# A decoder block in split fp32: left sides of the first products and value weights moved, output projection in order, three gate and up products begun ahead

## The chip, the core and the metric

The kernel runs on one core of one Trainium2 chip. The core has five engines with an instruction queue each: TensorE (PE, matrix products), VectorE (DVE), ScalarE (ACT), GpSimd (POOL) and SyncE (SP), which here issues nearly all DMAs. Each engine takes its instructions strictly in the order in which they were issued; semaphores make it wait for the others. The metric is the device time of one execution in microseconds (us), lower is better.

## What is computed

One layer of a decoder block on 1024 tokens of width 1024, all in float32:

```
h = rmsnorm(x, norm_mix)
qa, ka, va, qb, fb, ib, gb, gate_a, gate_b = split(h @ w_in)
ya = dilated_attention(qa, ka, va)              # 8 heads of 64, three windows
yb = hgrn2(qb, fb, ib, gb, lb, hg_norm)         # 4 heads, chunks of 64
x = x + (sigmoid(gate_a) * (ya @ w_a_up) + sigmoid(gate_b) * (yb @ w_b_up)) @ w_out
g, u = split(rmsnorm(x, norm_ffn) @ w_gu)       # 2 x 2816 wide
x = x + (silu(g) * u) @ w_down
x = x + (p @ w_pe) * sigmoid(rmsnorm(x, norm_ple) @ w_pg)
out = rmsnorm(x, norm_final)
```

## The kernel before

**Numbers.** Every float32 operand of a matrix product is split into a high and a low part (a cast to fp32r, and the difference). A product of two such operands is three matmuls: hi with hi, hi with lo, lo with hi. A split of a weight or an activation is a cast on ACT (or on POOL for `wr`, in `weight`) and a subtraction on DVE.

**Units.** Most projections (10 units) and gate and up (22 units) use Strassen's scheme in Winograd's form, in `winograd`. A unit covers two blocks of weights; it has seven products, always in the order 1, 5, 7, 2, 3, 4, 6, each of 12 matmuls with 512 columns (four blocks of the contraction, three matmuls for each). The generator `lefts` loads a unit's two weights (`w0`, `w1`, on SP), builds the sums s1 to s4 and splits the seven left sides into `q` (cast L299, difference L300); a pool of five buffers lets it run that far ahead. The right sides are made once, from the activations, and are used by all units: `right_b11` (product 1), `right_t1` (5), `right_t3` (7), `right_b21` (2), `right_b22` (3), `right_t4` (4), `right_t2` (6). Each of them ends in `block`: a cast on ACT (L235) and a difference on DVE (L236). T3 needs a difference on POOL (L249), T2 another (L261), T1 and T4 one on DVE (L245, L262). In PSUM a unit's products share banks: product 2 is added to the bank of product 1, after ACT has copied product 1 to `m` (L333), and DVE reads a bank for the sums `v` and `u` (L335, L337) before the next use of it.

**The program in time.** (1) The start, up to 56 us: the activation x arrives in eight tiles `xr`, is scaled by the norm's gains and split (`xh`, `xl`), and its squares are summed in `sqs`; meanwhile five tiles of gates are computed directly (`start`). The norm's factor is `rstd_rep`: an fp32 matmul of `ones` with the sums into a bank (`ms`, L209), two reads of this bank by ACT (L210, L211; the first needs its table of functions), three steps on DVE. (2) The ten projection units, 56 to 264 us; their right sides are made by `start_rights`, which first scales `xr` in place (L376). (3) Attention, from 264 us: queries and keys come back from DRAM (`qr`, `kl`) and are split (`q`, `kh`, `kl`); the value product is `v_gemm` (L484 to L486), with weights `wr` split to `wh` and `wl`; scores are `sp` (L525, L526), their row maxima come from DVE (L538), the exponential from ACT (L542). A `Filler` puts steps of gate products between the scores. (4) The recurrence, the merge. (5) The output projection, to 875 us: for each of eight blocks d it computes x1, writes it, scales it to `xg`, and makes the right sides of gate and up as they become possible. (6) Gate and up, 22 units of some 19 us. Beside them SP, DVE and `down_sums` prepare left sides of the down projection (`ls`, stored to `s_dram`). (7) The down projection, (8) the last stage.

**What sets the order.** Code is written stage by stage, and a scheduler of the tile framework merges it to one order for each engine; `tc.issue_after(i)` holds what is recorded inside it behind the instruction i. Memory is given by numbered slots: `ring([41])` is a buffer in slot 41, and a new tile in it waits until the readers of the old one are done.

## Time and profile before

| | |
|---|---|
| median of three runs | 1650.5 us (1648.26 to 1650.99) |
| the profiled execution, its own time | 1653.13 us |
| its span, first to last instruction | 1651.3 us |
| busy: PE, DVE, ACT, POOL | 97%, 68%, 39%, 29% |
| mean granted clock of PE | 0.987 of full |
| read from and written to HBM | 164.16 and 62.39 MB |

The span is that of one profiled execution; all times inside it count from its start. A busy share is a mean over all stages: what a change in one stage is worth is read from that stage. A waiting PE is seen by the idle time ahead of one of its instructions, with the instruction of another engine that released it. The granted clock is the share of the full 2.4 GHz that PE was given in a stretch; its two levels are 1.0 and 0.5 (1.2 GHz).

### The profile page before, as it was taken

What the parts mean: (1) busy time and instruction counts of PE and PEld (TensorE: products, weight loads), DVE (VectorE), ACT (ScalarE), POOL (GpSimd) and SP (SyncE); (2) the same over time, 40 slices, a digit from 0 to 9 for tenths busy, and PEclk for the clock granted to TensorE, in tenths of its full rate; (3) what the DMA queues carried; (4) which work ended last, traced back from release to release, by engine and by line L of the source; (5) the groups of instructions that cost most, each with busy time, mean ns of one, the idle gap of its engine ahead of it and who ended that gap; (6) DMA issues with size and microseconds to landing.
All of it is one profiled execution on the core that took longest, in us unless ns stands there. A gap on an engine that the chain in (4) does not pass through costs nothing.

```text
span 1651.3 us, 21727 instructions
## 1 busy us (share of the span) xinstructions
PE 1599.5 (97%) x7968; PEld 1334.9 (81%) x7968; DVE 1119.2 (68%) x1725; ACT 651.9 (39%) x1130; POOL 475.7 (29%) x357
## 2 busy tenths in 40 slices
PE   8899998999999999999998999999999999999996
PEld 7687776898897888888786878888888788878886
DVE  8855655568665567774648786667777757789536
ACT  6422333357653011532336333333333454454433
POOL 2555662223322111015353222223333201002214
PEclk9999998999999999999999999999999999999998
DMA  5233344223224232543434773224444677765102
GB/s 199 77 103 113 128 147 140 80 87 81 65 71 156 91 108 98 177 145 118 134 127 144 269 260 130 90 101 142 153 160 159 214 262 249 237 200 159 43 1 102
DMA packets 93419, 227.97 MB, mean 138 GB/s; under 512 B 10368, under 2 KB 19840, under 8 KB 93312
## 3 DMA queue, kind: packets, MB, share of 16 engines
q1 hardware_dynamic: 93168, 226.57, 41.3%
q8 instruction: 62, 1.02, 0.3%
q14 instruction: 45, 0.37, 0.1%
q10 hardware_dynamic: 144, 0.02, 0.0%
HBM read 164.16 MB, written 62.39 MB: 137 GB/s over the span
## 4 chain that ended last, share of the span: by engine, by line
PE 47%; DVE 6%; DMA 5%; issue 2%; POOL 1%; ACT 1%; SPq 0%; DVEq 0%; POOLq 0%
PE u L275 7%; PE u L276 7%; PE u L277 7%; PE mm L192 5%; PE mm L194 5%; PE mm L193 5%; PE dnb L275 2%; PE dnb L277 2%; PE dnb L276 2%; DVE B L236 1%; DMA s_dram<-ls 1%; PE g L666 1%; DMA ls<-w_dn 1%; DMA w<-s_dram 1%; DMA w<-w_dn 1%
## 5 line engine op out<-in xcount | busy, mean ns | idle before, releaser
L275 PE MATMUL u<-B,q 128*128 128x512 f32 x776 | 303.9, 394 | 8.3 <-ACT m L333 5.1
L276 PE MATMUL u<-B,q 128*128 128x512 f32 x776 | 304.3, 392 | 3.9 <-DVE B L236 3.9
L277 PE MATMUL u<-B,q 128*128 128x512 f32 x776 | 303.6, 391 | 2.9 <-DVE q L300 2.9
L275 PEld LDWEIGHTS u<-B,q 128*128 128x128 f32 x776 | 146.8, 189 | 44.1 <-ACT m L333 9.5
L276 PEld LDWEIGHTS u<-B,q 128*128 128x128 f32 x776 | 146.6, 189 | 35.3 <-DVE B L236 5.4
L277 PEld LDWEIGHTS u<-B,q 128*128 128x128 f32 x776 | 146.7, 189 | 34.1 <-DVE q L300 3.3
L192 PE MATMUL mm<-xh,wh 128*128 128x512 f32 (+1 forms) x352 | 138.6, 394 | 0.0
L299 ACT CAST q<-s 128x512 fp32r<-128x512 f32 x128 | 79.4, 622 | 148.9 <-PE u L277 132.9
L300 DVE TENSOR_TENSOR q<-s,q 128x512 fp32r<-128x512 f32 x128 | 107.3, 841 | 40.9 <-ACT q L299 40.1
L194 PE MATMUL mm<-xh,wl 128*128 128x512 f32 (+1 forms) x352 | 132.3, 376 | 0.1
L193 PE MATMUL mm<-xl,wh 128*128 128x512 f32 (+1 forms) x352 | 131.8, 374 | 0.0
L171 POOL TENSOR_SCALAR wh<-wr 128x1024 fp32r<-128x1024 f32 (+1 forms) x55 | 59.9, 1091 | 247.6 <-PE mm L193 104.7
L300 DVE TENSOR_TENSOR q<-w,q 128x512 fp32r<-128x512 f32 x96 | 91.9, 958 | 51.1 <-ACT q L299 51.0
L192 PE MATMUL mm<-h,wh 128*128 128x512 f32 (+1 forms) x296 | 114.7, 387 | 1.2 <-POOL wh L171 1.1
L193 PE MATMUL mm<-l,wh 128*128 128x512 f32 (+1 forms) x296 | 114.4, 386 | 0.9 <-DVE l L910 0.9
L194 PE MATMUL mm<-h,wl 128*128 128x512 f32 (+1 forms) x296 | 113.7, 385 | 0.0
L299 ACT CAST q<-w 128x512 fp32r<-128x512 f32 x96 | 59.7, 622 | 122.0 <-PE u L277 69.7
L544 POOL TENSOR_SCALAR p<-p,rd 128x128 f32<-128x128 f32 (+3 forms) x64 | 53.3, 835 | 143.3 <-DVE rd L543 123.8
L1103 POOL TENSOR_TENSOR us<-v 128x512 f32<-128x512 f32 x22 | 38.4, 1746 | 171.6 <-DVE v L337 158.7
L194 PEld LDWEIGHTS mm<-xh,wl 128*128 128x128 f32 x352 | 66.8, 190 | 12.0 <-DVE wl L172 0.5
L484 PE MATMUL mm<-wh,xh 128*128 128x256 f32 x256 | 76.4, 300 | 0.0
L294 POOL TENSOR_TENSOR s<-s,w 128x512 f32<-128x512 f32 x32 | 45.1, 1410 | 107.4 <-DVE s L292 88.2
(305 smaller groups left out, 3791.5 us busy)
## 6 DMA issues: line engine op xcount, KB each, us to landing
w<-w_gu SPq DMA_DIRECT2D x44, 512.0 KB, 3.9
t_dram<-t SPq DMA_DIRECT2D x44, 256.0 KB, 2.3
w<-w_in SPq DMA_DIRECT2D x20, 512.0 KB, 3.8
w<-w_dn SPq DMA_DIRECT2D x40, 256.0 KB, 3.3
st<-t_dram SPq DMA_DIRECT2D x20, 512.0 KB, 4.5
ls<-w_dn SPq DMA_DIRECT2D x32, 256.0 KB, 4.1
wr<-w_in SPq DMA_DIRECT2D x13, 512.0 KB, 3.7
sg_dram<-gt SPq DMA_DIRECT2D x24, 256.0 KB, 2.0
```

The lines of the kernel that those rows point to most:

```text
L171: pool.tensor_scalar(hi, raw, 1.0, 0.0, ALU.mult, ALU.add)
L192: pe.matmul(dst, hi[:, k, :], xh[:, c0 : c0 + n], start=first and k == ks[0], stop=False)
L193: pe.matmul(dst, hi[:, k, :], xl[:, c0 : c0 + n], start=False, stop=False)
L194: pe.matmul(dst, lo[:, k, :], xh[:, c0 : c0 + n], start=False, stop=last and k == ks[-1])
L275: pe.matmul(dst, q[:, 0, k], bh, start=first and not more and k == 0, stop=False, skip_group_check=more)
L276: pe.matmul(dst, q[:, 0, k], bl, start=False, stop=False, skip_group_check=more)
L277: pe.matmul(dst, q[:, 1, k], bh, start=False, stop=end, skip_group_check=more)
L294: pool.tensor_sub(s2, s1, a11)
L299: act.copy(q[:, 0], left[m])
L300: dve.tensor_sub(q[:, 1], left[m], f32(q)[:, 0])
L484: pe.matmul(b, xh[:, ts_], hi[:, k % 4, :], start=(k == 0), stop=False)
L544: pool.tensor_scalar(pr[:, :n], pr[:, :n], rd, 0.0, ALU.mult, ALU.add)
```

## The change

Five things are changed; all matmuls of products are the same.

1. At the start ACT scales all eight `xr` in a row, and the right sides of product 5 and of product 7 are made behind them, with POOL's differences for T2 directly between and behind those for T3. The norm's `rstd_rep` is recorded after these, behind `right_read` and `right_made`.
2. The first value weights `w_v0` are loaded and split during the last projection unit, in slots 41 to 44. The first pair of score rows is held behind the last matmul of the first value product (`values_made`).
3. The output projection takes its blocks d in the order 0 to 7 rather than 0, 4, 1, 5, 2, 6, 3, 7. For d under 4 the right sides of products 1 and 5 are made, for the others that of 7 and T2's difference, and the squares follow behind POOL's last instruction.
4. Gate and up's left sides are pinned ahead of the right sides of products 2, 3, 4 and 6 (`ffn_lead`), with product 1's left side of the second unit taken third (`early`). Products 1 and 5 of the first unit and product 1 of the second are issued before product 7.
5. The norm's two sums for gate and up go to a bank of their own tag, `b1`.

```diff
@@ -276,16 +276,29 @@
...
             pe.matmul(dst, q[:, 1, k], bh, start=False, stop=end, skip_group_check=more)
-    def winograd(units, qr, sr, after=(), eng=pool):
+    def winograd(units, qr, sr, after=(), eng=pool, early=False):
         def lefts():
-            for src0, src1, n in units:
-                w0, w1 = RAW.next([P, 2 * n, P], F32, "w0"), RAW.next([P, 2 * n, P], F32, "w1")
-                nc.sync.dma_start(w0, src0)
-                nc.sync.dma_start(w1, src1)
+            def load(src, n, name):
+                w = RAW.next([P, 2 * n, P], F32, name)
+                nc.sync.dma_start(w, src)
+                return w
+            def split_left(x, n):
+                q = qr.next([P, 2, n, P], F32R, "q")
+                act.copy(q[:, 0], x)
+                dve.tensor_sub(q[:, 1], x, f32(q)[:, 0])
+                return q
+            second = None
+            for i, (src0, src1, n) in enumerate(units):
+                w0 = second if early and i == 1 else load(src0, n, "w0")
+                w1 = load(src1, n, "w1")
                 a11, a12, a21, a22 = w0[:, :n], w0[:, n:], w1[:, :n], w1[:, n:]
@@ -294,11 +307,11 @@
...
                 left = {1: a11, 2: a12, 3: s4, 4: a22, 5: s1, 6: s2, 7: s3}
-                for m in ORDER:
-                    q = qr.next([P, 2, n, P], F32R, "q")
-                    act.copy(q[:, 0], left[m])
-                    dve.tensor_sub(q[:, 1], left[m], f32(q)[:, 0])
-                    yield q
+                for m in ORDER[1:] if early and i == 1 else ORDER:
+                    yield split_left(left[m], n)
+                    if early and i == 0 and m == ORDER[1]:
+                        second = load(units[1][0], n, "w0")
+                        yield split_left(second[:, :n], n)
         left_gen, ahead, unit_gen = chain(lefts(), after), [], iter(enumerate(units))
@@ -360,7 +373,7 @@
...
     for _ in range(WARM):
-        pe.matmul(warm[:, :P], ones, ones, start=True, stop=True)
+        warm_up = pe.matmul(warm[:, :P], ones, ones, start=True, stop=True)
     w_start = [weight_parts(a["w_in"][20 + t], [P, KD, P]) for t in range(NTOGETHER)]
@@ -372,9 +385,10 @@
     def start_rights(j, i):
-        for k in {5: (i,), 7: (i + 4,)}.get(j, ()):
-            act.activation(xr8[k], xr8[k], AF.Identity, scale=vec[:, V_MIX + k : V_MIX + k + 1])
-        right[j][i] = RIGHT[j](xr8, i, 4, ring([TB[j][i]]))
+        t2 = (xr8[i + 4][:, c1],) if j in (4, 6) else ()
+        right[j][i] = RIGHT[j](xr8, i, 4, ring([TB[j][i]]), *t2)
+    pe_engine, pool_engine = warm_up.ins.engine, nc.gpsimd.engine
     def latest(engine):
@@ -416,19 +430,31 @@
...
             dve.tensor_copy(lmask, lm)
-    rs = ring([46]).next([P, S], F32, "rs")
-    t1, t2 = TMP.next([P, S], F32, "t"), TMP.next([P, S], F32, "t")
-    for c in range(2):
-        cs = slice(c * 512, c * 512 + 512)
-        scale_read, _ = rstd_rep(rs[:, cs], sqs[:, cs], MS.next([P, 512], F32, "ms"), 1.0 / D, t1[:, cs], t2[:, cs])
     with tc.issue_after(last_sum.ins):
...
     with tc.issue_after(last_split), tc.issue_after(last_square.ins):
+        for k in range(KD):
+            act.activation(xr8[k], xr8[k], AF.Identity, scale=vec[:, V_MIX + k : V_MIX + k + 1])
+        scaled = latest(act_engine)
+    with tc.issue_after(scaled):
+        for j in (5, 7):
+            for i in range(4):
+                start_rights(j, i)
+            right_read, right_made = latest(act_engine), latest(last_sum.ins.engine)
         for i in range(4):
-            start_rights(5, i)
+            t2 = xr8[i + 4][:, c1]
+            pool.tensor_sub(t2, t2, xr8[i][:, c0])
+    rs = ring([46]).next([P, S], F32, "rs")
+    t1, t2 = TMP.next([P, S], F32, "t"), TMP.next([P, S], F32, "t")
+    with tc.issue_after(right_read), tc.issue_after(right_made):
+        for c in range(2):
+            cs = slice(c * 512, c * 512 + 512)
+            bank = MS.next([P, 512], F32, "ms")
+            scale_read, _ = rstd_rep(rs[:, cs], sqs[:, cs], bank, 1.0 / D, t1[:, cs], t2[:, cs])
     banks.append([ps.tile([P, 512], F32, tag=t, name=f"start_{t}") for t in ("pt1", "pt0")])
@@ -486,8 +512,8 @@
...
             yield 3 * 0.107
-    def v_gemm(half, vs):
-        wts = [weight(a["w_v"][half, j], [P, 4, 256]) for j in range(2)]
+    def v_gemm(half, vs, wts=None):
+        wts = wts or [weight(a["w_v"][half, j], [P, 4, 256]) for j in range(2)]
         for t in range(NTOK):
@@ -751,11 +777,8 @@
...
     with tc.issue_after(latest(last_sum.ins.engine)), tc.issue_after(scale_read.ins):
-        for i in range(4):
-            start_rights(7, i)
-        for i in (3, 0, 1, 2):
-            for j in (4, 6):
-                start_rights(j, i)
+        for j, i in ((4, 3), (6, 3), (4, 0), (4, 1), (4, 2), (6, 0), (6, 1), (6, 2)):
+            start_rights(j, i)
     TG, EO = ring([37, 38, 39]), ring([40, 47, 8])
@@ -766,6 +789,9 @@
...
     for tiles in units:
+        if tiles == units[-1]:
+            w_v0 = [weight(a["w_v"][0, j], [P, 4, 256], ring([41 + j]), ring([43 + j])) for j in range(2)]
         done = dict(proj_unit(right, TG))
@@ -843,12 +869,14 @@
...
     nc.sync.dma_start(NB, a["nb"])
-    drain(v_gemm(0, vs[0]))
+    drain(v_gemm(0, vs[0], w_v0))
+    values_made = latest(pe_engine)
     RAW, HI, LO = ring([0, 1]), ring([3, 4]), ring([8, 6])
...
     v_last = fill.add(v_gemm(1, vs[1]))
-    fill.along(attend_rows(0, qk[0, 0], rows), SCALE_A)
+    with tc.issue_after(values_made):
+        fill.along(attend_rows(0, qk[0, 0], rows), SCALE_A)
     groups = [(p, h, g) for p in range(NPAIR) for h in range(2) for g in range(2)]
@@ -957,7 +985,7 @@
...
     xs, right = [None] * KD, {j: [] for j in ORDER}
-    for d in (0, 4, 1, 5, 2, 6, 3, 7):
+    for d in range(KD):
         x = XS.next([P, S], F32, "x1")
@@ -974,16 +1002,16 @@
...
             act.activation(g[:, cs], x[:, cs], AF.Identity, scale=vec[:, V_FFN + d : V_FFN + d + 1])
-        for j in ORDER[:2] if d < 4 else ORDER[2:3]:
+        for j in (1, 5) if d < 4 else (7,):
             right[j].append(RIGHT[j](xs, d % 4, 4, SLOTS[j]))
         if d >= 4:
-            f = xs[d - 4]
-            pool.tensor_sub(f[:, c0], g[:, c1], f[:, c0])
-        for c, cs in enumerate(halves):
-            square(d, c, x[:, cs], sums, RS2, pool)
-    for j in ORDER[3:]:
-        t2 = [(xs[i][:, c0],) if j in (4, 6) else () for i in range(4)]
-        right[j] = [RIGHT[j](xs, i, 4, SLOTS[j], *t2[i]) for i in range(4)]
+            t2 = xs[d - 4][:, c0]
+            with tc.issue_after(latest(pool_engine)):
+                last_t2 = pool.tensor_sub(t2, g[:, c1], t2)
+        with tc.issue_after(last_t2.ins if d == KD - 1 else latest(pool_engine)):
+            for c, cs in enumerate(halves):
+                square(d, c, x[:, cs], sums, RS2, pool)
@@ -1046,8 +1074,8 @@
...
     T, QR = ring([29, 30, 31, 34, 8]), ring(range(3, 8))
-    ffn_unit, next_left, _ = winograd(
-        [(a["w_gu"][2 * ft], a["w_gu"][2 * ft + 1], 4) for ft in range(NF)], QR, ring([47, 48]), down_lefts(), dve
+    ffn_unit, next_left, ffn_lead = winograd(
+        [(a["w_gu"][2 * ft], a["w_gu"][2 * ft + 1], 4) for ft in range(NF)], QR, ring([47, 48]), down_lefts(), dve, early=True
     )
@@ -1065,13 +1093,23 @@
...
                 yield
+    ffn_lead()
+    with tc.issue_after(latest(act_engine)), tc.issue_after(latest(last_sum.ins.engine)):
+        for j in (2, 3, 4, 6):
+            t2 = [(xs[i][:, c0],) if j in (4, 6) else () for i in range(4)]
+            right[j] = [RIGHT[j](xs, i, 4, SLOTS[j], *t2[i]) for i in range(4)]
+    g0, g1 = ffn_unit(right, T), ffn_unit(right, T)
+    begun = [next(g0), next(g0)], [next(g1)]
+    first_units = [chain(begun[0], g0), chain(begun[1], g1)]
     rs, down_right = None, {n: [] for n in range(len(DOWN_ORDER))}
...
             ahead = down_rights(0, down_right[0])
-        for j, r in ffn_unit(right, T):
+        for j, r in first_units.pop(0) if first_units else ffn_unit(right, T):
             done[j] = r
@@ -1083,7 +1121,10 @@
...
             t = ring([33]).next([P, 2, 512], F32, "t")
-            token_scale(rs, sums, [t[:, 0], t[:, 1]])
+            for c in range(2):
+                bank = ps.tile([P, 512], F32, tag="b1", name=f"ms{c}")
+                rstd_rep(rs[c], sums[c], bank, 1.0 / D, t[:, 0], t[:, 1])
             gs = T.next([P, S], F32, "gs")
```

**ACT at the start.** Rows of ACT's order from the first scaling of `xr` on. `xr<-xr,vec` is the scaling, `B` a right side's cast, `ms` the norm's bank, `q` a unit's left side; L376 before is L441 in the change. Before:

```order
L376 ACTIVATE xr_207<-xr_207,vec 128x1024
L235 CAST B_374<-xr_110 128x512
L235 CAST B_379<-xr_147 128x512
L235 CAST B_384<-xr_177 128x512
L235 CAST B_389<-xr_207 128x512
L210 ACT_TABLE_LOAD
L210 ACTIVATE rs_349<-ms_352,eps 128x512
L211 ACTIVATE t_350<-ms_352,eps 128x512
L210 ACTIVATE rs_349<-ms_359,eps 128x512
```

And now:

```order
L441 ACTIVATE xr_322<-xr_322,vec 128x1024
L235 CAST B_364<-xr_110 128x512
L235 CAST B_368<-xr_147 128x512
L235 CAST B_372<-xr_177 128x512
L235 CAST B_376<-xr_207 128x512
L235 CAST B_380<-xr_110 128x512
L235 CAST B_384<-xr_147 128x512
L235 CAST B_388<-xr_177 128x512
L235 CAST B_392<-xr_207 128x512
L210 ACT_TABLE_LOAD
L210 ACTIVATE rs_399<-ms_402,eps 128x512
L211 ACTIVATE t_400<-ms_402,eps 128x512
```

The last scaling here is that of the eighth tile (the fourth in before), and the four casts of T3 (B_380 to B_392) have moved ahead of the table load and the reads of `ms`.

**PE from the last projection unit to attention.** `u` is a projection product, `mm` with L484 or L510 the value product, `sp` scores. Before:

```order
L277 MATMUL u_1812<-B_528,q_1848 128x512
L484 MATMUL mm_1976<-wh_1965,xh_111 128x256
L484 MATMUL mm_2003<-wh_1965,xh_111 128x256
L484 MATMUL mm_2031<-wh_1965,xh_111 128x256
L525 MATMUL sp_2195<-kh_1924,q_1923 128x256
L526 MATMUL sp_2195<-kl_1925,q_1923 128x256
L525 MATMUL sp_2217<-kh_1924,q_1923 128x256
```

Now, behind the 192 matmuls of the value product (its last two, the scores, and a gate's `mm_2213`):

```order
L511 MATMUL mm_2168<-wl_1820,xh_323 128x256
L512 MATMUL mm_2168<-wh_1819,xl_324 128x256
L551 MATMUL sp_2195<-kh_1936,q_1935 128x256
L552 MATMUL sp_2195<-kl_1937,q_1935 128x256
L192 MATMUL mm_2213<-xh_111,wh_2208 128x512
L193 MATMUL mm_2213<-xl_112,wh_2208 128x512
L194 MATMUL mm_2213<-xh_111,wl_2209 128x512
L551 MATMUL sp_2217<-kh_1936,q_1935 128x256
```

The scores have moved from the third matmul of the value product to behind its last, and alternate with three matmuls of a gate.

**DVE at the start of gate and up**, in the change: `q` are lo parts of left sides, `s34` a unit's sums, `w1_1015` the second weight of the third unit, `v_990` the sum whose reading of u_986 frees the bank that the norm's first sum takes.

```order
L295 TENSOR_TENSOR q_1003_7663<-s34_1001_7643,q_1003_7663 128x512
L1038 TENSOR_TENSOR ls_1045_7993<-ls_1045_7993 128x512
L295 TENSOR_TENSOR q_1004_7678<-w0_965_7505,q_1004_7678 128x512
L295 TENSOR_TENSOR q_1005_7693<-s34_1001_7643,q_1005_7693 128x512
L306 TENSOR_TENSOR s34_1017_7778<-w0_1014_7773,w1_1015_7775 128x512
L350 TENSOR_TENSOR v_990_7573<-u_986_7569,m_989_7572 128x512
```

The third unit's L306 stands here ahead of L350; PE's rows of the same place have `ms0` four matmuls after the last product of the first unit, where the two sums stood between product 7 and product 2 before.

## Rows read from the trace of the kernel before

**Rows 1.** The page: PE's share, and a DMA group (KB, us to landing).

```profile
PE 1599.5 (97%) x7968; PEld 1334.9 (81%) x7968; DVE 1119.2 (68%) x1725; ACT 651.9 (39%) x1130; POOL 475.7 (29%) x357
...
w<-w_gu SPq DMA_DIRECT2D x44, 512.0 KB, 3.9
```

**Rows 2.** PE's waits by line and releaser: us in total, times, longest.

```profile
PE u L275 <- ACT m L333: 5.1, 3, 2.3
...
PE dnb L275 <- ACT q L1044: 1.7, 1, 1.7
PE sp L525 <- DVE m L538: 1.6, 3, 0.7
```

**Rows 3.** Windows: length, busy us of each engine, granted clock, DMA.

```profile
56.29:85.65 29.36, 23.19 (x85) 17.31 (x84) 27.79 (x31) 12.28 (x21) 16.50 (x10) 0.88 0.26 90
264.45:280.66 16.21, 9.31 (x32) 6.70 (x31) 11.58 (x23) 6.48 (x14) 6.90 (x6) 0.58 0.64 194
875.47:888.25 12.78, 8.35 (x32) 5.37 (x30) 10.97 (x17) 8.92 (x18) 6.21 (x3) 1.00 0.25 87
888.25:910.00 21.75, 21.75 (x95) 17.70 (x96) 21.44 (x34) 11.89 (x18) 4.92 (x3) 1.00 0.62 204
1450.54:1455.00 4.46, 4.42 (x11) 2.92 (x12) 4.46 (x8) 2.03 (x4) 0.17 (x1) 0.62 0.62 221
```

**Rows 4.** Timeline of PE, start and first unit: start, us, instruction, [idle before <-releaser].

```profile
47.48 1.02 PE L209 MATMUL ms<-sqs,ones 128*128 128x512 f32 x2
...
65.35 0.59 PE L276 MATMUL u<-B,q 128*128 128x512 f32 x1 [3.04 <-DVE B L236]
...
78.87 0.50 PE L277 MATMUL u<-B,q 128*128 128x512 f32 x1 [2.89 <-DVE q L300]
```

**Rows 5.** Timelines of ACT, POOL and DVE, 35 to 67 us.

```profile
35.65 1.83 ACT L235 CAST B<-xr 128x512 fp32r<-128x512 f32 x3 [3.62 <-DVE xr L245]
...
39.96 1.28 ACT L210 ACT_TABLE_LOAD   x1
...
45.30 0.68 ACT L211 ACTIVATE t<-ms,eps 128x512 f32<-128x512 f32 x1
...
53.52 1.30 POOL L249 TENSOR_TENSOR xr<-xr,xr 128x512 f32<-128x512 f32 x1 [1.94 <-ACT xr L376]
...
64.83 1.60 POOL L261 TENSOR_TENSOR xr<-xr,xr 128x512 f32<-128x512 f32 x1
...
39.98 0.69 DVE L236 TENSOR_TENSOR B<-xr,B 128x512 fp32r<-128x512 f32 x1 [0.74 <-ACT B L235]
...
52.78 1.88 DVE L439 TENSOR_TENSOR gt<-start_b,rs 128x512 f32<-128x512 f32 x3
```

**Rows 6.** Timeline of PE at the first scores.

```profile
267.40 0.58 PE L525 MATMUL sp<-kh,q 128*128 128x256 f32 x1 [2.45 <-ACT kh L472]
```

**Rows 7.** Timelines of POOL and SP, 254 to 266 us; loads of tile kl.

```profile
254.79 1.05 POOL L171 TENSOR_SCALAR wh<-wr 128x1024 fp32r<-128x1024 f32 x1 [3.80 <-PE u L277]
...
261.80 3.25 SPq L465 DMA_DIRECT2D kl<-qk_dram  x4
...
DMA to landing us min/median/max: 3.7/4.0/4.3
```

**Rows 8.** Timeline of PE, first unit of gate and up.

```profile
882.40 0.50 PE L275 MATMUL u<-B,q 128*128 128x512 f32 x1 [2.01 <-ACT B L235]
...
888.25 0.50 PE L275 MATMUL u<-B,q 128*128 128x512 f32 x1 [1.80 <-ACT m L333]
```

**Rows 9.** Timelines of POOL, ACT and SP, 878 to 896 us.

```profile
878.41 3.29 POOL L249 TENSOR_TENSOR xg<-xg,xg 128x512 f32<-128x512 f32 x1 [4.40 <-ACT xg L976]
...
881.73 2.70 ACT L235 CAST B<-xg 128x512 fp32r<-128x512 f32 x5 [2.37 <-POOL xg L249]
...
895.39 0.33 SPq L1008 DMA_DIRECT2D ls<-w_dn  x1
```

**Rows 10.** Timeline of PE, fourth unit of gate and up.

```profile
952.39 0.50 PE L275 MATMUL u<-B,q 128*128 128x512 f32 x1 [1.26 <-DVE v L335]
```

## Prediction

> **What bounds the kernel now.** The page comes first: TensorE (PE) is busy 97% of the span [rows 1], so only a stretch in which PE stands still or runs slowly can be won. The table of PE's waits is next. It says for each line which engine ended the wait: the largest sum is 5.1 us in three waits, and most of the others are single waits of 1 to 3 us [rows 2]. PE's timeline shows where they stand: the larger ones lie in three short stretches, and those are what the change rewrites. The table by windows then gives, for a stretch, its length, PE's matmuls and the granted clock [rows 3]; a wait costs more than its length where the clock falls to 1.2 GHz behind it.
>
> The pace: 95 matmuls of 512 columns in 21.75 us at a clock of 1.00 [rows 3], 0.229 us each, 2.75 for a product of 12.
>
> *Stretch A, the first projection unit*, from its product 1 (56.29) to that of unit 1 (85.65): 29.36 us at a clock of 0.88 for 84 matmuls, 19.2 us of work [rows 3]. **10.1 us are lost**, most of it in waits of 3.04 and 2.89 us [rows 4] and the low clock behind both. A chain stands behind them. ScalarE (ACT) scales the last four xr only after the norm. GpSimd (POOL), which needs them for T3 and T2, makes its eight differences from 53.52 to 66.43, 1.61 us each [rows 5]. Product 7's right sides wait for these, and the left side that is late at 78.87 stands on VectorE (DVE) behind their lo parts.
>
> *Stretch B, from the last projection unit to attention*: 16.21 us at a clock of 0.58 [rows 3], with 22 matmuls of 256 columns (0.115 each), eight of scores and a transposition, 3.8 us of work at full pace. **12.4 us are lost.** PE issues three matmuls of the value product, turns to the scores, waits 2.45 us for kh [rows 6] and then for kl, the maxima and wl, and goes on at half clock.
>
> *Stretch C, from the output projection to gate and up*: 12.78 us [rows 3] for 26 matmuls (5.95 us) and two of the norm's sums (0.9 each by the two passes of 1.02, which overlap [rows 4]). **5.0 us are lost**, at full clock, most of it in waits of 2.01 us on the last T3 block and 1.80 on ACT's copy m [rows 8].
>
> The waits elsewhere have instructions whose order the change leaves; they stay.
>
> **Part A of the change: left sides scaled first, T3 and T2 moved ahead.** ACT scales all eight xr in a row. POOL can begin when DVE's first T1 difference is out, which is when ACT's first cast starts in before, 35.65 [rows 5]. Product 7's right sides are then complete 13 us before that product starts, T2 has left POOL by 48.5, and the two waits go with the low clock behind them. What is added: ACT's order puts the norm's table load and its two reads of the ms bank behind the fourth T3 cast. That T3 is POOL's seventh operation. At 1.30 us each (the first) it ends at 44.75, at 1.61 (the mean beside a busy DVE) at 46.9 [rows 5]. A cast of 0.62, a table load of 1.28 and two reads of 0.68, pipelined to 1.3 [rows 5]: the bank is read by 47.9 to 50.1. The second ms matmul writes the same bank, and stands in PE's order at 47.48 [rows 4]; in before the read ended at 45.98. So PE gets a **new wait of 0.5 to 2.6 us**. I take 1.6, near the middle, since DVE works during part of POOL's operations only. Queued behind it are the matmuls of the fifth start tile, which nobody else awaits. The norm ends later too, by up to 3 us: the gate results that left their banks from 52.78 to 54.66 [rows 5] leave by 57.7 at the latest, and product 1, later by its own wait, asks at 58.9. If that cover were gone, it would cost what the norm is late beyond it. Gain: 10.1 − 1.6 = **8.5** (7.5 to 9.6).
>
> A rule speaks against this. Eight POOL operations took 12.91 us, 1.61 each where the first took 1.30 [rows 5], beside a DVE that was busy for 27.79 of 29.36 us [rows 3]. The Trainium skill, "SBUF — State Buffer", section "Who interferes with whom", says that the port pair shared by VectorE and GpSimd is an exclusive lock, and that the second comer "fully blocks" for the whole instruction. By that each POOL operation could stand behind a whole DVE operation; what this would give is rival 1.
>
> **Part B: first value weights moved, scores pinned behind the value product.** The weights go to slots 41 to 44, which hold T3's blocks and are free after product 7 of the last unit: the event at which POOL split wr in before, 254.79, after 3.80 us of waiting for PE [rows 7]. Two splits of 1.05 end by 256.9, DVE's lo parts by 258.2, six us before PE asks at 264.45. Behind them on DVE stands the last unit's sum v, which product 4 needs at about 259; it is close, and 0 to 0.5 us may be lost. The value product (192 matmuls of 256 columns, 22.0 us) then follows u without a wait and covers the loads of kl, issued from 261.80 to 265.05 and landing in 4.3 us at most [rows 7], and their casts. Every pair of scores has three matmuls of a gate behind it (0.69 us), which cover the waits on maxima (1.6 us in three [rows 2]) in large part. Left over I take 1.0 us, for the first exponential's table load and the maxima: 0.5 to 2, and 1.7 more if the clock falls (below). Gain: 12.4 − 1.0 = **11.4** (8.7 to 11.9).
>
> **Part C: output projection in order, three products begun ahead.** PE now does u0's products 1 and 5 and u1's product 1 (8.2 us) before u0's product 7. The T3 block that came at 882.40 is wanted only when product 7 reaches its last three matmuls, at 885.7, and POOL's outlier (3.29 us for one difference [rows 9]) is covered. Two new waits follow.
> - Product 2 comes at 886.4 into the bank of u0's product 1, which ACT must copy out first. The copy stands eleven entries behind the last T3 cast, which ran at 881.73; at 0.54 each (five in 2.70 [rows 9]) it ends at 888.2, two us sooner without the outlier, 0.7 later if a cast waits for DVE: **0 to 2.5, I take 1.5**.
> - ms0 comes at 898.2. It takes the bank that DVE's L350 must read, and L350 stands directly behind L306 s_1017, which needs the second weight of the third unit. SP issues that load behind an ls load that waits for stores to land, at 895.39 in before [rows 9]; the stretch is about 1 us ahead now, so 894.4. With 3.9 to land (median of w_gu [rows 1]) and two DVE steps of 0.69 [rows 5], 899.7: **0.9 to 4, I take 1.8**.
>
> Gain: 5.0 − 3.3 = **1.7** (−1.5 to 4.1).
>
> **The low clock.** Waits of the size of the three new ones (1.6, 1.5, 1.8) go both ways in before: behind 1.7 us at the down projection [rows 2] the clock was 0.62 for 4.46 us, which costs 1.7; behind 1.80 it stayed at 1.00 [rows 3, 8]. I let one of the three be followed by such a stretch: **−1.7** (0 to −3.4).
>
> Gate and up's later units, the down projection and the last stage keep their order but for a few neighbours: 0.
>
> **Sum.** 8.5 + 11.4 + 1.7 − 1.7 = 19.9. The profiled execution took 1653.13, so 1633.2. That run was 2.6 above the median of the three, 1650.5, and the stretches are the same in them: **1630.6**.
>
> **The rivals.**
> 1. *A gives half of it back.* If each of seven POOL operations also waited for a whole DVE operation: 35.65 + 7 × (1.30 + 0.69) = 49.6, the bank read at 52.8, PE waiting 5.3 instead of 1.6, and the clock falls: 3.7 + 1.7 = 5.4 more, **1636.0**. For it: ACT's table load now stands behind all of them, and one POOL operation has taken 3.29 us [rows 9]. Against it: the mean of 1.61 [rows 5]. By the Trainium skill's rule cited above this is how it goes; the trace's mean lies between.
> 2. *C turns into a loss.* A second weight that lands 3 us later holds DVE's whole queue, PE waits 5 at ms0 and the clock falls: 3.2 + 1.7 more, **1635.5**. For it: SP's queue is in order, and loads in it wait for stores [rows 9].
> 3. *B's waits only move.* If kh and kl were late at the scores again, 2.45 [rows 6], about 2 for kl and 1.6 come back with a low clock, 8 in all: **1638.6**. Against it: 22 us of cover for a landing of 4.3 [rows 7].
> 4. *Slower.* In gate and up PE waited 1.26 us for a sum v at 952.39 [rows 10]; ahead of v on DVE stood a sum that had waited for the unit's second weight. The change shifts SP's entries in these 22 units. At 1.26 in each of 20 units it costs 25 us: **1656**. It decides from 1.2 us a unit: (19.9 + 3.3) over 20. Against it: in the new order this load stands one to three entries ahead of where it stood.
> 5. *No difference*: other waits take the place of the old ones in A and B, so that under 3.3 us of their 19.9 are left: **1648 to 1653**. Against it: the operands named come earlier by more than the waits.
>
> **How the numbers follow.** Forecast 0.70, its own range 1625.5 to 1634.5; rivals 1 to 5: 0.12, 0.08, 0.03, 0.04, 0.03. All best ends together give 25.6 of gain (1624.9), all worst 11.3 (1639.2): from these the range, 1625 to 1639, which takes in rivals 1 to 3. A measurement of this kernel tells 0.2% (3.3 us) from no change: faster 0.93, same 0.03, slower 0.04.
>
> **What would show it.** A: no wait of u near 65 and 79 us, full clock there, unit 1's product 1 near 77, and one wait of ms on ACT near 47.5, under 2.7 us. B: no wait at the first mm behind u, full clock for 20 us, short waits at the first scores. C: none on the T3 block; one at product 2 on ACT's m, one at ms0 on DVE's v. The prediction is wrong if ms waits over 4 us, if the first scores wait for kl, or if a unit of gate and up takes over 20 us (seven products are 19.2).

## The result and the profile after

The changed kernel takes **1635.33 us** (median of 4 runs, 1634.44 to 1636.71), the kernel before 1650.74 on the same chip: a ratio of 0.991 [0.9897, 0.9922] (the 95% interval, here and behind every ratio), 15.4 us faster. The forecast was 1630.6, 19.9 faster. The profiled execution took 1635.94 us with a span of 1634.1; that of before took 1653.13 with 1651.3, so 17.2 us of span have to be found in the two traces.

The page, beside [rows 1], hardly moves: PE was busy 97% before and is now.

```profile
PE 1590.1 (97%) x7968; PEld 1330.1 (81%) x7968; DVE 1123.6 (69%) x1725; ACT 651.7 (40%) x1130; POOL 478.0 (29%) x357
```

The waits of PE by line and releaser (us in total, times, longest), beside [rows 2]: the largest single ones are new.

```profile
PE u L275 <- ACT m L346: 8.4, 4, 4.1
PE ms L209 <- ACT t L211: 5.1, 1, 5.1
```

The windows of the changed kernel show the three stretches (length, then busy us of PE, PEld, DVE, ACT and POOL, granted clock, DMA share, GB/s); [rows 3] has those of before.

```profile
49.64:55.66 6.02, 6.02 (x12) 4.07 (x13) 5.63 (x8) 3.85 (x7) 2.97 (x2) 0.51 0.00 0
61.34:80.38 19.04, 19.04 (x86) 15.77 (x84) 16.64 (x24) 8.97 (x16) 9.69 (x4) 1.00 0.31 110
258.56:285.07 26.51, 26.51 (x210) 25.73 (x209) 13.55 (x28) 9.85 (x20) 4.24 (x3) 1.00 0.45 137
871.80:875.07 3.27, 3.27 (x8) 2.61 (x9) 3.27 (x6) 0.73 (x2) 0.26 (x1) 0.56 0.78 241
856.64:1288.58 431.94, 423.90 (x1852) 347.41 (x1851) 321.93 (x448) 155.72 (x264) 123.33 (x77) 1.00 0.48 162
```

In the first unit, from its product 1 to that of the second unit, PE is now busy without a gap at full clock: 19.04 us where it was 29.36 [rows 3]. From the last unit into attention the same, 26.51 us without a gap. But ahead of the first unit, and in the first unit of gate and up, there is a stretch at half clock. Gate and up as a whole became *longer*. Its window in the kernel before:

```profile
875.47:1303.78 428.31, 422.62 (x1853) 346.24 (x1851) 318.06 (x448) 155.51 (x264) 121.31 (x76) 1.00 0.48 163
```

By these starts the 17.2 us divide so:

| Stretch | before | after | difference |
|---|---|---|---|
| start, to the first u | 56.29 | 61.34 | +5.1 |
| projection units, to the last u (264.22, 258.34) | 207.93 | 197.00 | −10.9 |
| values, attention, output projection | 611.25 | 598.30 | −12.9 |
| gate and up | 428.31 | 431.94 | +3.6 |
| the rest, to the end of the span | 347.5 | 345.5 | −2.0 |

The two executions did not start alike: PE's first matmul of `ms` stands at 43.66 in that of before and at 40.57 in this one, with the same work ahead of it. The first two rows hold this difference too.

**Stretch A.** The timeline of the changed kernel's start (start, us, instruction, idle time before and its releaser):

```profile
34.59 1.61 POOL L249 TENSOR_TENSOR xr<-xr,xr 128x512 f32<-128x512 f32 x1 [2.96 <-DVE xr L245]
...
44.66 1.70 POOL L249 TENSOR_TENSOR xr<-xr,xr 128x512 f32<-128x512 f32 x1
...
48.91 0.68 ACT L211 ACTIVATE t<-ms,eps 128x512 f32<-128x512 f32 x1
...
38.38 11.40 DVE L236 TENSOR_TENSOR B<-xr,B 128x512 fp32r<-128x512 f32 x8
...
49.64 2.07 PE L209 MATMUL ms<-sqs,ones 128*128 128x512 f32 x2 [5.09 <-ACT t L211]
...
61.34 0.39 PE L275 MATMUL u<-xh,q 128*128 128x512 f32 x1
```

PE came to the second ms matmul at 49.64 − 5.09 = 44.55 and stood until ACT had read the bank at 49.59. POOL's fourth T3 started at 44.66, six operations after 34.59: 1.68 us each. DVE's eight lo parts took 11.40 us, 1.43 each, where [rows 5] has one in 0.69.

**Stretch C**, in the same form:

```profile
859.00 3.25 POOL L249 TENSOR_TENSOR xg<-xg,xg 128x512 f32<-128x512 f32 x1 [5.79 <-ACT xg L1004]
...
863.46 3.45 POOL L975 TENSOR_TENSOR sums<-sums,sq 128x512 f32<-128x512 f32 x2
...
862.94 2.82 DVE L236 TENSOR_TENSOR B<-xg,B 128x512 fp32r<-128x512 f32 x2 [1.84 <-ACT B L235]
...
867.49 1.22 ACT L235 CAST B<-xg 128x512 fp32r<-128x512 f32 x2 [1.99 <-DVE xg L262]
...
871.16 1.07 ACT L346 COPY m<-u 128x512 f32<-128x512 f32 x2 [0.92 <-DVE B L236]
...
871.80 0.79 PE L275 MATMUL u<-B,q 128*128 128x512 f32 x1 [4.12 <-ACT m L346]
...
885.39 0.69 DVE L306 TENSOR_TENSOR s<-w,w 128x512 f32<-128x512 f32 x1 [2.32 <-DMA w<-w_gu]
...
886.83 1.10 PE L209 MATMUL ms<-sums,ones 128*128 128x512 f32 x2 [1.59 <-DVE v L350]
```

The T3 block no longer holds PE, and both new waits are where they were expected: at product 2 on the copy m, and at ms0 on v, behind an L306 that waits for its weight. The first is 4.12 long, though, because ACT's casts ahead of the copy waited for DVE, and the copy too (0.92, for the lo part that reads the slot it writes). DVE's two lo parts from 862.94 on took 2.82 us beside POOL's squares, where the six from 867.99 on, with POOL still, took 3.69. At product 2 begins the half-clock window above.

### The profile page after: what moved, and what is told of

It reads as the page before. It is cut to its first block, busy times and chain, and to the rows that moved or that the text cites. A ratio compares the mean times of both kernels' runs of the same rounds, so it can differ in the third digit from the quotient of the medians.

```text
span 1634.1 us, 21728 instructions
## 1 busy us (share of the span) xinstructions
PE 1590.1 (97%) x7968; PEld 1330.1 (81%) x7968; DVE 1123.6 (69%) x1725; ACT 651.7 (40%) x1130; POOL 478.0 (29%) x357
## 4 chain that ended last, share of the span: by engine, by line
PE 46%; DVE 7%; DMA 6%; issue 2%; ACT 1%; POOL 1%; SPq 0%; DVEq 0%; POOLq 0%; ACTq 0%
PE u L275 6%; PE u L276 6%; PE u L277 6%; PE mm L192 5%; PE mm L194 5%; PE mm L193 5%; PE dnb L275 1%; PE dnb L276 1%; PE dnb L277 1%; DMA s_dram<-ls 1%; DVE B L236 1%; DMA ls<-w_dn 1%; PE g L692 1%; POOL sb L954 1%; DMA st<-first_dram 1%
## 5 line engine op out<-in xcount | busy, mean ns | idle before, releaser
L194 PEld LDWEIGHTS mm<-xh,wl 128*128 128x128 f32 x352 | 66.8, 190 | 11.4
L510 PE MATMUL mm<-wh,xh 128*128 128x256 f32 x256 | 75.9, 297 | 0.0
```

What stands on the lines that cost most here:

```text
L194: pe.matmul(dst, lo[:, k, :], xh[:, c0 : c0 + n], start=False, stop=last and k == ks[-1])
L510: pe.matmul(b, xh[:, ts_], hi[:, k % 4, :], start=(k == 0), stop=False)
```

## The experiments

Each is compared with the kernel before on the same chip: 1650.28 us for the first four, 1650.09 for the next four, 1648.04 for three, 1649.81 for the last; the changed kernel's own 1635.33 stands beside 1650.74. The diffs are against the changed kernel.

**1. undo_start.** The order of the start goes back (part A alone undone).

```
-        for k in range(KD):
-            act.activation(xr8[k], xr8[k], AF.Identity, scale=vec[...])
-    with tc.issue_after(scaled):
-        for j in (5, 7): ... start_rights(j, i)     # and T2, ahead of rstd_rep
+    ... rstd_rep(...)                               # the norm first
+            start_rights(5, i)                      # scales xr i ahead of each
...
-        for j, i in ((4, 3), (6, 3), (4, 0), ...): start_rights(j, i)
+        for i in range(4): start_rights(7, i)       # in the first unit again
+        for i in (3, 0, 1, 2): ... for j in (4, 6): start_rights(j, i)
```

> The changed kernel with its start (scalings, T3 and T2, the norm's place) put back as before; value weights and output projection stay changed. First theory, from the two traces: the start saved 10.9 us in the first projection unit and gave back 8.0 in the new wait on the ms bank and the low clock behind it, so putting it back costs 2.9 us: 1638.2. Rival: the new wait was only this long because PE was 2.9 us early at that point in that one execution, so the start is worth 5.9: 1641.2. Second rival: the start is worth nothing or is a loss (1635.3 or less).

1640.07 us, 0.9944 [0.9929, 0.9959]: 4.7 more than the changed kernel, between the two figures. Its PE timeline:

```profile
53.22 0.39 PE L275 MATMUL u<-xh,q 128*128 128x512 f32 x1
...
62.29 0.51 PE L276 MATMUL u<-B,q 128*128 128x512 f32 x1 [3.04 <-DVE B L236]
...
75.79 0.50 PE L277 MATMUL u<-B,q 128*128 128x512 f32 x1 [2.20 <-DVE q L295]
```

and the window of its first unit:

```profile
53.22:81.07 27.85, 21.89 (x86) 16.56 (x84) 27.71 (x31) 12.28 (x21) 16.51 (x10) 0.94 0.26 96
```

The old waits are back, but the first product begins at 53.22, 8 us ahead of the changed kernel's. What A is worth depends on when PE comes. This execution and that of the changed kernel have the same early start (first `ms` matmul at 40.59 and 40.57), and the second unit begins at 81.07 here and at 80.38 there: A wins 0.7. With a late start it begins at 85.65 in the kernel before (43.66) and at 80.15 in experiment 3, which has the changed start (43.37): A wins some 5. In the six profiles with the changed start it begins between 79.19 and 81.07, whenever PE came. The medians, over executions whose starts mostly were not seen, give 4.7.

**2. undo_values** (part B alone undone: `w_v0` is loaded where it was, and the scores are not held behind the values).

```
-         if tiles == units[-1]:
-             w_v0 = [weight(a["w_v"][0, j], [P, 4, 256], ring([41 + j]), ring([43 + j])) for j in range(2)]
-    drain(v_gemm(0, vs[0], w_v0))
+    drain(v_gemm(0, vs[0]))
-    with tc.issue_after(values_made):
```

> The changed kernel with the value weights loaded where they were and the first score rows not held back. First theory: the stretch gained 12.9 us by itself, so 1635.3 + 12.9 = 1648.2, with waits on kh, kl and wl and a half clock back at its place. Rival: part of the gain was taken from later attention rows, which then run earlier, and less than 9 us come back: under 1644.

1646.91 us, 0.9986 [0.9975, 0.9998]: B is worth 11.6, nearer to the first theory's 12.9 than to the rival's less than 9. From the last u to gate and up lie 610.2 us here and 598.3 in the changed kernel, 11.9 less. The earlier load and the held scores are undone together; which of them brings it is not separated. The waits at the scores and the low clock come back together, in PE's timeline

```profile
260.68 0.39 PE L551 MATMUL sp<-kh,q 128*128 128x256 f32 x1 [2.31 <-DVE pj L803]
...
263.48 0.58 PE L552 MATMUL sp<-kl,q 128*128 128x256 f32 x1 [2.41 <-DVE kl L501]
```

and in the window over it:

```profile
257.86:275.00 17.14, 10.05 (x41) 7.53 (x40) 11.71 (x23) 6.80 (x15) 6.89 (x6) 0.70 0.61 187
```

**3. undo_output** (part C alone undone: the output tiles in the old order, no products begun ahead, the norm's bank as before).

```
-    for d in range(KD):
+    for d in (0, 4, 1, 5, 2, 6, 3, 7):
-        for j in (1, 5) if d < 4 else (7,):
+        for j in ORDER[:2] if d < 4 else ORDER[2:3]:
-    ffn_lead()
...
-    begun = [next(g0), next(g0)], [next(g1)]
```

> The changed kernel with the output projection and the start of gate and up put back as before. First theory: that part lost 3.6 us between the end of the output projection and the end of gate and up (4.12 and 1.59 of new waits, low clock, against 5.0 before), so 1635.3 - 3.6 = 1631.7. Rival: the waits there are a matter of the DMAs' phase in one execution and the part is worth its 1.7 us, so 1637.0.

1634.42 us, 0.9904 [0.9889, 0.9919]: no difference from the changed kernel that can be told, so C is worth nothing, if it is not a small loss. Gate and up is 3.0 us shorter than in the changed kernel, with one wait of 3.35 for a lo part in place of 4.12 and 1.59. The stretch behind it is 1.2 longer (345.5 there, 346.7 here, to the end of the span of 1633.4), which tells nothing: in the 14 profiles of this study it lies between 343.5 and 348.5, and none of the edits touches its code.

```profile
857.73:1286.68 428.95, 424.24 (x1852) 347.12 (x1851) 319.13 (x448) 156.08 (x264) 119.84 (x76) 1.00 0.48 163
```

The run also shows A in an execution whose start came later. Its POOL, ACT and PE:

```profile
35.45 1.62 POOL L249 TENSOR_TENSOR xr<-xr,xr 128x512 f32<-128x512 f32 x1 [2.97 <-DVE xr L245]
...
45.52 1.74 POOL L249 TENSOR_TENSOR xr<-xr,xr 128x512 f32<-128x512 f32 x1
...
49.80 0.68 ACT L211 ACTIVATE t<-ms,eps 128x512 f32<-128x512 f32 x1
...
50.54 1.53 PE L209 MATMUL ms<-sqs,ones 128*128 128x512 f32 x2 [3.19 <-ACT t L211]
...
61.11 0.39 PE L275 MATMUL u<-xh,q 128*128 128x512 f32 x1
```

and two windows, behind the wait and of the first unit:

```profile
50.54:56.50 5.96, 5.96 (x17) 4.26 (x18) 5.57 (x8) 3.95 (x7) 3.51 (x2) 0.71 0.00 0
61.11:80.15 19.04, 19.04 (x85) 15.77 (x84) 17.26 (x26) 8.96 (x16) 9.85 (x4) 1.00 0.37 134
```

Here PE came to ms at 47.35, as the prediction had assumed, and the wait is 3.19 instead of 5.09; the first product begins at 61.1 all the same.

**4. norm_before_t3.** T3's right sides wait for the norm's reads, so that ACT reads the ms bank first.

```
+    ... rights 5, then rstd_rep(...)
+        for i in range(4):
+            with tc.issue_after(scale_read.ins):
+                start_rights(7, i)
```

> The changed kernel with the norm's table load and reads of the ms bank ahead of ACT's four T3 casts (behind T1's); POOL's eight differences stay where they are. First theory (ACT's order makes the wait): PE's wait of 5.09 us on the ms bank and the half clock behind it go, 8.0 us in all: 1627.3, and product 7 still finds its operands. Rival (the operands of product 7 are then late instead): a wait on T3's blocks comes back, under 3 us are won: 1632.3 or more.

1635.32 us, 0.9913 [0.99, 0.9927]: no gain. The wait on ms is gone, but T3's lo parts now stand on DVE ahead of the gate evictions, and product 1 waits for a bank:

```profile
54.64 1.89 DVE L236 TENSOR_TENSOR B<-xr,B 128x512 fp32r<-128x512 f32 x3
...
57.27 0.77 PE L275 MATMUL u<-xh,q 128*128 128x512 f32 x1 [3.19 <-DVE gt L468]
```

**5. t3_first.** POOL makes its four T3 differences in a row, T2 behind them.

```
+        with tc.issue_after(latest(pool_engine)):
             for i in range(4): ... pool.tensor_sub(t2, ...)
```

> The changed kernel with POOL's four T3 differences ahead of its four T2 differences; nothing else moves. First theory (the read of the ms bank stands behind POOL's seventh operation, and product 1 starts at 61.3 us however early PE was): the fourth T3 is then POOL's fourth operation, done 5 us sooner, at 41.4; the bank is read by 44.6, PE's wait of 3.2 to 5.1 and the half clock go: 6 to 8 us, 1628. Rival (as in the run with the norm ahead of T3, the gates' results leave their banks late and product 1 waits for these): under 2 us, 1634.

1637.86 us, 0.9923 [0.9906, 0.9939]: slower than the changed kernel, if anything. The POOL and DVE rows say why:

```profile
39.51 13.66 DVE L236 TENSOR_TENSOR B<-xr,B 128x512 fp32r<-128x512 f32 x8
...
35.73 6.71 POOL L249 TENSOR_TENSOR xr<-xr,xr 128x512 f32<-128x512 f32 x4 [2.96 <-DVE xr L245]
...
42.41 6.82 POOL L451 TENSOR_TENSOR xr<-xr,xr 128x512 f32<-128x512 f32 x4
...
58.97 0.47 PE L275 MATMUL u<-xh,q 128*128 128x512 f32 x1 [2.79 <-DVE gt L466]
```

POOL takes 1.68 and 1.71 us for a difference whatever their order. DVE's lo parts now keep the same step, 13.66 / 8 = 1.71, so the norm's steps behind them are late. What binds this stretch is DVE, slowed while POOL works: the theory that only POOL's order mattered fell.

**6 to 8. copy_slot, copy_first, t3_and_copy_first.** The copy m gets a slot that no lo part reads; then the begun products also stand ahead of the last right sides; then both with experiment 5.

```
-    T, QR = ring([29, 30, 31, 34, 8]), ring(range(3, 8))
+    T, QR = ring([8, 30, 31, 29, 34]), ring(range(3, 8))
# copy_first also, ahead of the rights 2, 3, 4 and 6:
+    g0 = ffn_unit(right, T)
+    begun0 = [next(g0), next(g0)]
```

> The changed kernel with the first unit's copy m of gate and up in a slot that nothing reads any more (8 in place of 29; the order of the ring changes, and with it the scheduler puts the copy two entries earlier on ACT). First theory (the copy that product 2 waits 4.12 us for is late because of its place in ACT's queue and the readers of its slot): product 2 starts without a wait; product 3 then waits some 2 us for its left side, behind DVE's lo parts: 2 to 4 us won, 1632. Rival (the stretch is bound by DVE's sixteen or so operations between the last T3 cast and the end of the lo parts): the wait moves to products 3 and 4 whole, 1635.

> The changed kernel with the same slot, and with the first two products of gate and up recorded ahead of the right sides of products 2, 3, 4 and 6, so that their copies and product 3's left side stand right behind the last T3 cast on ACT; on SP the third unit's second weight comes ahead of the down projection's loads, and on DVE the sum v that ms0 waits for ahead of that unit's sum. First theory: both new waits (4.12 and 1.59) and the half clock go: 6 to 7 us, 1629. Rival (DVE bounds the stretch): 2 us at most, 1633.5.

> Both repairs, T3 ahead of T2 and the copies first. If the parts add: 1635.3 - 7 - 6.5 = 1621.8. If each only moves its wait: 1633 or more.

1637.53 [0.9902, 0.9938], 1635.44 [0.9889, 0.9923] and 1638.04 us [0.9911, 0.9941] (ratios 0.992, 0.9906, 0.9926). The wait at product 2 goes or shrinks (0.60 in copy_first), and others come, in copy_slot

```profile
871.89 0.50 PE L277 MATMUL u<-B,q 128*128 128x512 f32 x1 [1.47 <-DVE q L295]
...
884.14 0.69 DVE L306 TENSOR_TENSOR s<-w,w 128x512 f32<-128x512 f32 x1 [2.40 <-DMA w<-w_gu]
...
885.58 1.86 PE L209 MATMUL ms<-sums,ones 128*128 128x512 f32 x2 [4.74 <-DVE v L350]
```

and in copy_first

```profile
879.25 0.79 PE L277 MATMUL u<-B,q 128*128 128x512 f32 x1 [2.15 <-DVE q L295]
```

All three end on DVE, but at ms0 DVE itself had stood 2.40 us for the third unit's weight. copy_slot's runs lie from 1633 to 1641, so its loss is not settled; that there is no gain is.

**9 to 11. differences_on_dve, slot_and_sum, both_repairs.** In the first, T3's and T2's differences at the start move to DVE (T2 into the first unit). In the second, with copy_slot's ring, the first sum of the late second weight moves to POOL. The third is both.

```
-        pool.tensor_sub(f[i][:, c1], f[i + n][:, c1], f[i][:, c1])
+        diff.tensor_sub(f[i][:, c1], f[i + n][:, c1], f[i][:, c1])   # diff = dve for j == 7
...
-                eng.tensor_sub(s3, a11, a21)
+                (pool if early and i == 2 else eng).tensor_sub(s3, a11, a21)
```

> The changed kernel with the eight differences of T3 and T2 at the start computed by VectorE instead of GpSimd: T3's in the place where they were, T2's behind the gates' results. Theory so far (VectorE bounds this stretch, and while GpSimd works each of its operations lets VectorE do one only, in 1.7 us rather than 0.6): eight operations more on VectorE, 4.8 us, against some 8 to 9 us of blocked time less; the lo parts take 0.6 each, the ms bank is read by 46.2, product 1 starts at 54 to 56 instead of 61.3, and the first unit keeps its length: 5 to 7 us, 1629. Rival (VectorE is full anyway, what counts is the number of its operations): product 1 later or the first unit longer, no gain: 1635 or more.

> The run with the copy in slot 8, and the third unit's sum s3 moved from VectorE to GpSimd, so that VectorE's v for ms0 does not stand behind a load any more. Theory: ms0's wait of 4.74 and the low clock behind it go, product 2's too; 1.5 at product 3 is left: 5 to 6 us, 1629.5. Rival (the wait is VectorE's backlog, not the load): the 4.7 stay in large part, 1635 or more.

> The two together. If they add: 1635.3 - 6 - 5.5 = 1624. If one of them only moves its wait: 1629; if both do: 1635.

1636.35 [0.9913, 0.9938], 1633.99 [0.9898, 0.9925] and 1632.87 us [0.9892, 0.9919] (0.9925, 0.9912, 0.9905): against their own kernel before, no more than the change alone. With the differences on DVE the start is as theory had it, the lo parts at 0.61 each and the first product at 55.99; the gain is lost again in the first unit, 25.06 us long to the second unit's first product where it was 19.04:

```profile
38.82 4.30 DVE L236 TENSOR_TENSOR B<-xr,B 128x512 fp32r<-128x512 f32 x7
...
55.99 0.39 PE L275 MATMUL u<-xh,q 128*128 128x512 f32 x1
...
64.72 7.59 POOL L305 TENSOR_TENSOR s<-w 128x512 f32<-128x512 f32 x1 [13.23 <-ACT B L235]
...
74.87 0.80 PE L275 MATMUL u<-B,q 128*128 128x512 f32 x1 [2.90 <-DVE v L348]
```

A POOL sum took 7.59 us beside a DVE that ran without pause; a cast waited 3.52 for it, and through DVE's queue the sum v that PE needs. In slot_and_sum POOL's sum at 877.02 took 4.63 us in the same way, and ms0 waits 1.68 again.

**12. t2_on_gpsimd_late.** both_repairs, with T2 on POOL again, behind its sums of the first unit.

```
+        with tc.issue_after(latest(pool_engine)):
+            for i in (3, 0, 1, 2): ... pool.tensor_sub(t2, t2, xr8[i][:, c0])
```

> The run with both repairs, with T2's four differences back on GpSimd, but behind its own sums for the first unit (from about 51.5 us on, while VectorE empties the gates' banks). Theory (VectorE's run of operations without a pause from 60 to 71 us kept GpSimd from its L305 for 7.6 us, and ACT, VectorE's lo part and sum v stood behind it): that run is four operations shorter, L305 is done some 2 us sooner, and PE's wait of 2.90 on v in the first unit shrinks to 1 or less: 2 to 4 us, 1630. Rival (T2 on GpSimd holds VectorE or is itself held there): product 1 or product 6 late instead, no gain: 1633 or more.

**1628.84 us**, 0.9882 [0.9863, 0.99]: the best version, 21 faster than before. Against the changed kernel it wins 6.5 by the medians, 5.6 by the gains over each chip's own kernel before; the two intervals just overlap. PE waits 1.86 at ms and 1.45 at 57.40, both at full clock, the first product begins at 55.34, and no wait on v follows in the first unit:

```profile
47.35 0.69 DVE L205 SCALAR_TENSOR_TENSOR rs<-t,rs 128x512 f32<-128x512 f32 x1
...
51.48 1.67 DVE L205 SCALAR_TENSOR_TENSOR rs<-t,rs 128x512 f32<-128x512 f32 x1
53.07 1.87 DVE L463 TENSOR_TENSOR gt<-start_b,rs 128x512 f32<-128x512 f32 x3
...
50.86 5.93 POOL L781 TENSOR_TENSOR xr<-xr,xr 128x512 f32<-128x512 f32 x4
...
55.34 0.39 PE L275 MATMUL u<-xh,q 128*128 128x512 f32 x1
```

T2's four take 1.48 us each here, mostly beside DVE evictions (gt) that still take about 0.62. Two things differ from both_repairs, the engine of T2 and, with it, DVE's order (v stands ahead of the last lo part there); which of them ended the wait on v is not separated.

## Why the prediction was right, and where it was off

The time lies in the stated range of 1625 to 1639, but 0.8 above the forecast's own, which ends at 1634.5. B came as forecast; A and C gave less.

The undo runs give each part on its own scale, medians against medians: A 4.7, B 11.6, C −0.9. They add to 15.4, the whole difference. Taken as gains over each chip's own kernel before, they are 5.2, 12.0 and −0.4, 16.8 in all. Each is the difference of two figures that are sure to some 2.5 us, so this shows no more than that no large share of the gain needs two parts together.

- **B, 11.4 forecast, 11.6 measured.** The waits it named are gone: none at the first value product, full clock, scores without gaps in the window 258.56:285.07. The 1.0 us left over for maxima and the table load was not spent. The place called close, DVE's v in the last unit, cost a wait of 0.66 at 251.17 (0 to 0.5 was allowed).
- **A, 8.5 forecast, 4.7 measured.** The two waits of [rows 4] are gone, as forecast. The term that failed is "I take 1.6" for the new wait on ms: 3.19 where PE came at the assumed time, 5.09 where it came 2.9 us earlier, beyond the prediction's own sign of being wrong (over 4 us). Two steps led to it. The first is the bound of 1.30 to 1.61 for a POOL operation: six took 1.68 each in both executions, and the bank was read at 50.5 in the later one, where 47.9 to 50.1 was forecast. The second step is 47.48 for PE's arrival, which was one execution's: over the 14 profiles of this study the first ms matmul starts between 40.57 and 43.66, though nothing ahead of it changed, and the chain over DVE, POOL and ACT doesn't follow (0.86 of 2.8 between these two), so an early start is lost in the wait. Behind it came half clock: 6.02 us at 0.51, or 5.96 at 0.71, costing 2.9 and 1.7. With the later execution's numbers A is 10.1 − 3.19 − 1.7 = 5.2, near what undo_start gives. The right price stood in the kernel before, where 1.61 is a mean over two kinds: the first two of the eight operations took 1.30 each beside gate evictions, the six from 56.16 to 66.43 took 1.71 each beside DVE's lo parts. Seven at 1.71 and the 3.2 us behind them give 50.8 for the bank's reading, so a wait of 3.3.

```profile
56.16 1.74 POOL L249 TENSOR_TENSOR xr<-xr,xr 128x512 f32<-128x512 f32 x1
...
56.67 3.48 DVE L300 TENSOR_TENSOR q<-s,q 128x512 fp32r<-128x512 f32 x2
```

- **C, 1.7 forecast, −0.9 measured.** The waits' places and releasers were right. The copy's wait, "0 to 2.5, I take 1.5", was 4.12: the sum let ACT run its eleven entries at their own pace, 0.7 more if a cast waited for DVE, but ACT waited for DVE for 2.9 us in the two rows shown. ms0 lost 1.59 where 1.8 was forecast, and that is luck. Counted from the start of gate and up, which is 18.83 us earlier here, PE was due at ms0 at 879.4 and v at 880.9. They came at 885.2 and 886.7: the weight's load was issued at 880.82, 5 us later than forecast, and PE had lost 4.12 and 1.4 ahead of it. In copy_slot, where PE doesn't lose the 4.12, the wait at ms0 is 4.74. The sum added two waits of which the first shortens the second.
- **The low clock, "one of the three".** Two of three: behind 5.09 and 4.12, not behind 1.59. The second costs 3.27 × (1 − 0.56) = 1.4.
- **The later units, 0.** The stretch behind gate and up became 2.0 us shorter in the profiled executions, less than it varies by (343.5 to 348.5 in the 14 profiles).
- **The rivals.** Rival 1 (1636.0, a wait of 5.3) came nearest for A in size, but not by its sum: POOL's step is 1.68, not 1.30 + 0.69. What it had right is that DVE and POOL hold each other up; the larger share falls on DVE (0.69 to 1.43, and 1.71 in t3_first), which the prediction never priced. Rival 2's late weight is real, but the copy's wait hid it; copy_slot shows its size (4.74, where 5 was said). That the figures of both lie within 0.7 of the measured time is chance: each lets one part alone fall short, and both did. Rivals 3, 4 and 5 did not occur: the scores run without gaps, gate and up is 3.6 longer and not 25, and the operands of A and B were in time.

A fell short because DVE and POOL slow each other: with T3's and T2's differences off POOL (differences_on_dve, PE as late) the bank is read at 46.95 instead of 50.5 and the first product begins at 55.99 instead of 61.1, though the first unit takes this back. For C the same is argued from rows only, since no run moves POOL's squares, and a late weight stands beside it. Experiments 4 to 8, which only reorder work or its slots, move the wait and win nothing that can be told; number 12, which takes T3 from POOL, puts T2 beside evictions and has both edits of slot_and_sum, wins some 6 us more (5.6 to 6.5).

## What to carry to other kernels

Price a difference on GpSimd by what it does to VectorE as well: here it cost the two engines 1.7 us each where VectorE alone needs 0.6, so work beside PSUM evictions or none at all was the better place. When a wait is removed by moving work earlier, follow the queue that becomes last (here POOL's seventh difference, with the casts and the table load behind it) and take its arrival against the earliest start that PE has, not against the one profiled. Take an operation's price from rows with the same company, not from a mean over several. Where PE works for 97% of the span, a new wait of 4 us must be priced with the half-clock stretch behind it (here 1.4 to 2.9 us).

## What the runs showed of the hardware

- VectorE and GpSimd held each other up, operation by operation. A lo part on DVE took 0.61 us in a row of seven with POOL still (differences_on_dve), 1.71 in a row of eight beside POOL's eight (t3_first); L205 took 0.69 and, beside POOL, 1.67 in one run. POOL's difference took 1.30 [rows 5] and 1.68 to 1.71. The Trainium skill, "SBUF — State Buffer", section "Who interferes with whom", says that a DVE instruction with two SBUF inputs contends with a GpSimd instruction that reads SBUF, and that one with at most one SBUF input, outside DVE's two-port modes, does not. These rows agree: the gt evictions, one input of which is a PSUM bank, stayed at about 0.62 beside POOL.
- Where both ran long rows they went in step (13.66 for eight beside 13.53 for eight). Where DVE ran a row without pause beside a single operation of POOL, POOL's took 3.25, 4.63 and 7.59 us, and was done 1.1 to 1.2 us after DVE's row.
- Behind PE's waits of 5.09, 4.12 and 3.19 us the granted clock was 0.51, 0.56 and 0.71 over the 3.3 to 6.0 us shown, so at half for most of it; behind 1.59 it stayed at 1.00. Waits of about 2 us went both ways: 1.00 over 75.79:80.00 behind 2.20 (undo_start), 0.50 over 879.25:883.00 behind 2.15 (copy_first).
